# A gated broadcast on one core: input loads regrouped over two DMA queues, and one token shared between two engines

## The chip, the core and the metric

The kernel runs on one core of a Trainium2 chip. The metric is the device time of one execution, in microseconds (us), lower is better. Five runs of the kernel before took 93.67 to 93.85 us, with a median of 93.70 us.

## What is computed

```python
gate_weights = gate_weights / (np.sum(gate_weights, axis=-1, keepdims=True) + 1e-8)
output = x[:, :, None, :] * gate_weights[:, :, :, None]      # float32
```

`x` is 8 x 256 x 512 (4.2 MB), `gate_weights` is 8 x 256 x 8 (64 KB), and the output is 8 x 256 x 8 x 512 (33.6 MB). Every token's vector of 512 numbers is written out eight times, each time scaled by one normalised gate. There is one multiplication for every number that is written, and the output is eight times as large as the input.

## The kernel before

**Tiling.** The 2048 tokens are spread over 128 partitions, 16 tokens (`j` = 0 to 15) in each. "Token 3" below means the fourth token of every partition, 128 tokens in all. `x_all` holds all of x, `g_all` all gates, `gn` the normalised gates. `ring` is a buffer of 10 slots; a slot holds one finished token, 8 x 512 numbers in each partition.

**Loads (L46 to L48).** ScalarE's queue carries the gates. SyncE's queue carries x in two transfers: the head (tokens 0 to HEAD-1, with HEAD = 5, so 10,240 bytes in each partition), and then the rest (22,528 bytes in each partition). A queue issues its transfers in the order of the code. The profile calls SyncE's queue q1 and ScalarE's q10.

**Gates (L53 to L56).** VectorE sums the eight gates of each token, adds 1e-8, takes the reciprocal and multiplies. All work on tokens needs `gn`.

**Tokens (L70 to L87).** `CHUNKS` lists five chunks as (first token, number of tokens, first slot): tokens 0-1, 2-4, 5-7, 8-11 and 12-15. For each chunk the tokens are computed and one output transfer (L87) is issued on SyncE's queue. These transfers are called out1 to out5; they carry 4.2, 6.3, 6.3, 8.4 and 8.4 MB. A token is computed in one of three ways:

- tokens 0 and 1 are shared: three of the eight products on ScalarE (L63, 128x512 each) and five on VectorE (L65, 128x512 each);
- the first token of every later chunk (2, 5, 8, 12) goes to ScalarE, as eight products (L63);
- every other token is one VectorE instruction (L68, 128x4096).

A framework places the waits and orders each engine's instructions. Each transfer has its own semaphore, and a product waits until the whole transfer that brings its x has landed. Tokens 8 to 11 reuse the slots 0 to 3, so they wait until out1 and out2 have landed; tokens 12 and 13 reuse the slots 6 and 7 and wait for out3. The order on VectorE is by instruction, not by chunk: tokens 14 and 15, whose slots are fresh, come ahead of tokens 10 and 11.

Of the kernel before, what the change touches and what calls it, by code (L numbers as in the profile page):

```python
# [1 line left out]

# [4 lines left out]

SLOTS = 10
HEAD = 5
CHUNKS = ((0, 2, 0), (2, 3, 2), (5, 3, 5), (8, 4, 0), (12, 4, 6))  # L10


@with_exitstack
def kernel(
    ctx: ExitStack,
    tc: tile.TileContext,
    x: bass.AP,
    gate_weights: bass.AP,
    out: bass.AP,
):  # L20
    nc = tc.nc
    P = 128

    B, S, D = x.shape
    E = gate_weights.shape[-1]
    J = B * S // P

    fp32 = mybir.dt.float32
    mult = mybir.AluOpType.mult

    x_v = x.flatten_outer_dims().rearrange("(p j) d -> p j d", p=P)
    g_v = gate_weights.flatten_outer_dims().rearrange("(p j) e -> p j e", p=P)
    out_v = out.rearrange("b s e d -> (b s) e d").rearrange(
        "(p j) e d -> p j e d", p=P
    )

    pool = ctx.enter_context(tc.tile_pool(name="pool", bufs=1))

    g_all = pool.tile([P, J, E], fp32)
    x_all = pool.tile([P, J, D], fp32)  # L40
    ring = pool.tile([P, SLOTS, E, D], fp32)
    gsum = pool.tile([P, J, 1], fp32)
    gn = pool.tile([P, J, E], fp32)
    warm = pool.tile([P, 1], fp32)

    nc.scalar.dma_start(out=g_all, in_=g_v)  # L46
    nc.sync.dma_start(out=x_all[:, 0:HEAD, :], in_=x_v[:, 0:HEAD, :])
    nc.sync.dma_start(out=x_all[:, HEAD:J, :], in_=x_v[:, HEAD:J, :])  # L48

    nc.vector.memset(warm, 0.0)  # L50
    nc.scalar.copy(out=warm, in_=warm)  # L51

    nc.vector.reduce_sum(out=gsum, in_=g_all, axis=mybir.AxisListType.X)  # L53
    nc.vector.tensor_scalar_add(out=gsum, in0=gsum, scalar1=1e-8)  # L54
    nc.vector.reciprocal(out=gsum, in_=gsum)  # L55
    nc.vector.tensor_tensor(  # L56
        out=gn, in0=g_all, in1=gsum.to_broadcast([P, J, E]), op=mult
    )

    def scale_one(engine, j, e, slot):  # L60
        o_ap, s_ap = ring[:, slot, e, :], gn[:, j, e : e + 1]
        if engine is nc.scalar:
            nc.scalar.mul(out=o_ap, in_=x_all[:, j, :], mul=s_ap)  # L63
        else:
            nc.vector.tensor_scalar_mul(out=o_ap, in0=x_all[:, j, :], scalar1=s_ap)  # L65

    def scale_token(j, slot):
        nc.vector.tensor_tensor(  # L68
            out=ring[:, slot, :, :],
            in0=x_all[:, j : j + 1, :].to_broadcast([P, E, D]),  # L70
            in1=gn[:, j, :].unsqueeze(2).to_broadcast([P, E, D]),
            op=mult,
        )

    for j0, m, s0 in CHUNKS:
        for i in range(m):
            j, slot = j0 + i, s0 + i
            if j < 2:
                for e in range(E):
                    on_act = e < 3  # L80
                    scale_one(nc.scalar if on_act else nc.vector, j, e, slot)
            elif i == 0:
                for e in range(E):
                    scale_one(nc.scalar, j, e, slot)
            else:
                scale_token(j, slot)
        nc.sync.dma_start(  # L87
            out=out_v[:, j0 : j0 + m, :, :], in_=ring[:, s0 : s0 + m, :, :]
        )


# [1 line left out]
_INS = ['x', 'gate_weights']  # L93
_OUTS = [((8, 256, 8, 512), 'float32')]


# [23 lines left out]
```

## Time and profile before

| what | value |
|---|---|
| median of 5 runs | 93.70 us |
| the profiled execution's own time | 93.70 us |
| its span | 91.9 us |
| VectorE busy | 48.6 us (53%), 25 instructions |
| ScalarE busy | 25.1 us (27%), 40 instructions |
| bytes moved by DMA | 37.81 MB, mean 411 GB/s over the span |
| head of x landed (16 DMA engines) | 6.04 to 6.50 us |
| gates landed | 6.21 to 6.67 us |
| rest of x landed | 12.71 to 13.18 us |
| out1, out2, out3 landed (last of 16) | 23.14, 37.67, 52.21 us |
| out4, out5 landed (last of 16) | 71.75, 91.10 us |

Times are counted from the start of the span; 1.8 us of the execution's time lie outside it. A transfer is split over 16 DMA engines. Each of them moves its 8 partitions as 8 packets, one for each partition, and then sends a small packet that counts the landing. A transfer has landed when all 16 have. The trace holds a record of every packet, with its queue, its start and its duration; where the text speaks of packets, it reads those records.

### The profile page before, as it was taken

How to read it: one execution, taken by the hardware profiler on the slowest of the kernel's cores; microseconds unless marked ns; L12 is line 12 of the kernel's file. 1: busy time of each engine (PE TensorE's matmuls, PEld its weight loads, DVE VectorE, ACT ScalarE, POOL GpSimd, SP SyncE). 2: the span in 40 equal slices, each digit the busy share in tenths (PEclk: the TensorE clock that was granted, in tenths of full speed). 3: DMA queues.
4: the chain of work that ended last, by engine and by line, in shares of the span. 5: the costliest groups of instructions: out<-in, count | busy, mean ns of one | idle time of the engine just before them, and what ended most of it. 6: DMA issues, size and time to landing. Idle time of an engine off the chain costs nothing.

```text
span 91.9 us, 131 instructions
## 1 busy us (share of the span) xinstructions
DVE 48.6 (53%) x25; ACT 25.1 (27%) x40; POOL 0.2 (0%) x4
## 2 busy tenths in 40 slices
DVE  0009999999999999999999396000000000000000
ACT  5105999993892000000000299000000000000000
POOL 0000000000000000000000000000000000000000
DMA  3899989999778977997797999999982999999990
GB/s 54 355 494 402 392 385 456 456 456 570 342 342 385 642 342 342 578 449 342 342 684 342 456 456 456 456 456 456 456 371 114 428 456 456 456 456 456 456 456 0
DMA packets 1152, 37.81 MB, mean 411 GB/s; under 512 B 128, under 2 KB 256, under 8 KB 256
## 3 DMA queue, kind: packets, MB, share of 16 engines
q1 hardware_dynamic: 1008, 37.75, 95.9%
q10 hardware_dynamic: 144, 0.07, 0.3%
HBM read 4.26 MB, written 33.55 MB: 411 GB/s over the span
## 4 chain that ended last, share of the span: by engine, by line
DMA 31%; DVE 23%; ACT 5%; issue 2%; ACTq 1%; SPq 0%
DMA out_dram<-ring 25%; DVE ring L68 17%; DMA g_all<-in_gate_weights_dram 6%; ACT ring L63 5%; DVE ring L65 4%; ACTq L115 1%; DVE gn L56 0%; DVE gsum L53 0%; DVE gsum L55 0%; DVE gsum L54 0%; ACTq L63 0%; SPq L87 0%
## 5 line engine op out<-in xcount | busy, mean ns | idle before, releaser
L68 DVE TENSOR_TENSOR ring<-x_all,gn 128x4096 f32<-128x4096 f32 x10 | 43.5, 4419 | 1.4 <-DMA out_dram<-ring 1.4
L63 ACT ACTIVATE ring<-x_all,gn 128x512 f32<-128x512 f32 x38 | 23.6, 708 | 31.1 <-DMA out_dram<-ring 25.8
L65 DVE TENSOR_SCALAR ring<-x_all,gn 128x512 f32<-128x512 f32 x10 | 4.0, 480 | 0.0
L53 DVE TENSOR_REDUCE gsum<-g_all 128x16 f32<-128x128 f32 x1 | 0.3, 286 | 5.8 <-DMA g_all<-in_gate_weights_dram 5.8
L51 ACT ACT_TABLE_LOAD x1 | 1.3, 1283 | 1.1 <-PEq L104 1.1
L50 DVE MEMSET warm<- 128x1 f32 x1 | 0.1, 59 | 0.8 <-PEq L104 0.8
L56 DVE TENSOR_TENSOR gn<-g_all,gsum 128x128 f32<-128x128 f32 x1 | 0.3, 293 | 0.0
L55 DVE RECIPROCAL gsum<-gsum 128x16 f32<-128x16 f32 x1 | 0.3, 253 | 0.0
L51 ACT COPY warm<-warm 128x1 f32<-128x1 f32 x1 | 0.2, 193 | 0.0
L54 DVE TENSOR_SCALAR gsum<-gsum 128x16 f32<-128x16 f32 x1 | 0.2, 175 | 0.0
L104 POOL MEMSET const-bfloat16-1.0<- 128x1 bf16 x1 | 0.1, 102 | 0.0
L104 POOL MEMSET const-uint8-127<- 128x1 uint8 x1 | 0.1, 102 | 0.0
L104 POOL MEMSET const-float32-0.0<- 128x1 f32 x1 | 0.1, 101 | 0.2 <-issue 0.2
L104 POOL MEMSET const-float32-1.0<- 128x1 f32 x1 | 0.1, 99 | 0.0
## 6 DMA issues: line engine op xcount, KB each, us to landing
out_dram<-ring SPq DMA_DIRECT2D x2, 6144.0 KB, 20.0
out_dram<-ring SPq DMA_DIRECT2D x1, 4096.0 KB, 11.2
x_all<-in_x_dram SPq DMA_DIRECT2D x1, 2816.0 KB, 12.0
x_all<-in_x_dram SPq DMA_DIRECT2D x1, 1280.0 KB, 5.8
g_all<-in_gate_weights_dram ACTq DMA_DIRECT2D x1, 64.0 KB, 6.0
out_dram<-ring SPq DMA_DIRECT2D x2, 27.3
```

Of the source, the lines that this page charges most:

```text
L50: nc.vector.memset(warm, 0.0)
L51: nc.scalar.copy(out=warm, in_=warm)
L53: nc.vector.reduce_sum(out=gsum, in_=g_all, axis=mybir.AxisListType.X)
L54: nc.vector.tensor_scalar_add(out=gsum, in0=gsum, scalar1=1e-8)
L55: nc.vector.reciprocal(out=gsum, in_=gsum)
L56: nc.vector.tensor_tensor(out=gn, in0=g_all, in1=gsum.to_broadcast([P, J, E]), op=mult)
L63: nc.scalar.mul(out=o_ap, in_=x_all[:, j, :], mul=s_ap)
L65: nc.vector.tensor_scalar_mul(out=o_ap, in0=x_all[:, j, :], scalar1=s_ap)
L68: nc.vector.tensor_tensor(out=ring[:, slot, :, :], in0=x_all[:, j : j + 1, :].to_broadcast([P, E, D]), in1=gn[:, j, :].unsqueeze(2).to_bro ...
L104: nc = _bacc.Bacc("TRN2", target_bir_lowering=False, num_devices=1)
L115: with _tile.TileContext(nc) as tc:
```

## The change

HEAD becomes 2. The gates go first on SyncE's queue, the head of x (now tokens 0 and 1, 4,096 bytes in each partition) goes on ScalarE's queue, and the rest (now 14 tokens, 28,672 bytes in each partition) goes on SyncE's queue behind the gates. Tokens 2 to 4, which were in the head, are now in the rest. Token 2 stays on ScalarE. Token 3, which was one VectorE instruction, becomes eight: two products on ScalarE and six on VectorE. Token 4 stays one VectorE instruction. Chunks, slots and output transfers are as they were.

```diff
-HEAD = 5
+HEAD = 2
...
-    nc.scalar.dma_start(out=g_all, in_=g_v)
-    nc.sync.dma_start(out=x_all[:, 0:HEAD, :], in_=x_v[:, 0:HEAD, :])
+    nc.sync.dma_start(out=g_all, in_=g_v)
+    nc.scalar.dma_start(out=x_all[:, 0:HEAD, :], in_=x_v[:, 0:HEAD, :])
     nc.sync.dma_start(out=x_all[:, HEAD:J, :], in_=x_v[:, HEAD:J, :])
...
                     scale_one(nc.scalar if on_act else nc.vector, j, e, slot)
+            elif j == 2:
+                for e in range(E):
+                    scale_one(nc.scalar, j, e, slot)
+            elif j == 3:
+                for e in range(E):
+                    scale_one(nc.scalar if e < 2 else nc.vector, j, e, slot)
             elif i == 0:
                 for e in range(E):
                     scale_one(nc.scalar, j, e, slot)
```

## The prediction, made before the changed kernel was timed

> **What bounds the kernel now.** I read the page's slices first, then the issues, then the packet records at the places where one transfer follows another.
>
> On the page, the DMA row of the slices, the queues and the issues:
>
> ```profile
> DMA  3899989999778977997797999999982999999990
> q1 hardware_dynamic: 1008, 37.75, 95.9%
> q10 hardware_dynamic: 144, 0.07, 0.3%
> out_dram<-ring SPq DMA_DIRECT2D x1, 4096.0 KB, 11.2
> x_all<-in_x_dram SPq DMA_DIRECT2D x1, 2816.0 KB, 12.0
> x_all<-in_x_dram SPq DMA_DIRECT2D x1, 1280.0 KB, 5.8
> g_all<-in_gate_weights_dram ACTq DMA_DIRECT2D x1, 64.0 KB, 6.0
> ```
>
> The DMA engines are full from the second slice to the last: SyncE's queue alone takes 95.9% of their time. VectorE (53%) and ScalarE (27%) have slack. A digit below 9 is mostly a packet straddling a slice, so a gap has to be looked for in the records. The chain of waits ends with ScalarE's last work at 57.3 us, which is misleading: out4 and out5 are queued by then and run for another 34 us.
>
> Timeline (start, duration, what):
>
> ```profile
> 0.72 0.39 ACTq L46 DMA_DIRECT2D g_all<-in_gate_weights_dram  x1
> 0.73 0.38 SPq L47 DMA_DIRECT2D x_all<-in_x_dram  x1
> 1.16 0.42 SPq L48 DMA_DIRECT2D x_all<-in_x_dram  x1
> 6.70 0.29 DVE L53 TENSOR_REDUCE gsum<-g_all 128x16 f32<-128x128 f32 x1 [5.84 <-DMA g_all<-in_gate_weights_dram]
> 7.84 13.60 ACT L63 ACTIVATE ring<-x_all,gn 128x512 f32<-128x512 f32 x22 [5.21 <-DVE gn L56]
> 7.84 4.05 DVE L65 TENSOR_SCALAR ring<-x_all,gn 128x512 f32<-128x512 f32 x10
> 11.81 39.10 DVE L68 TENSOR_TENSOR ring<-x_all,gn 128x4096 f32<-128x4096 f32 x9
> 11.98 45.69 SPq L87 DMA_DIRECT2D out_dram<-ring  x5
> ```
>
> The first output is issued at 11.98. The loads need the DMA engines until almost 13 us, so that issue is nearly hidden. The DMA view of 12.3 to 13.0 us in 40 slices shows by how little:
>
> ```profile
> GB/s 0 0 0 0 0 0 0 0 0 0 0 0 0 0 0 0 0 0 0 0 0 0 0 0 0 0 0 0 0 0 7490 5617 0 5617 1872 3745 1872 1872 1872 0
> DMA packets 32, 0.52 MB, mean 749 GB/s; under 512 B 16, under 2 KB 16, under 8 KB 16
> ```
>
> A packet counts in the slice where it starts. The sixteen small packets are the ends of the x load, from 12.35 to 12.82 us by the records; the sixteen large ones are the first of out1, starting at 12.83 to 12.98. So fifteen DMA engines idle for up to 0.5 us, and the sixteenth, done with x at 12.82, does not. From there every engine moves at its own fixed pace: 1.22 us for 32,768 bytes, 1.82 for 49,152, 2.42 for 65,536, each packet starting where the one before ends. One more gap follows: out3's last packets end at 51.68 to 51.86, and out4, issued at 50.98, begins at 51.84 to 51.98, again about 0.86 us behind its issue (to the first engine). Out2 and out5 are issued long ahead. The end is the latest engine's, so only what moves the latest engine counts.
>
> **The loads.** Bytes are unchanged. An engine's eight packets of the head repeat every 382 ns at 10,240 bytes, a 512-byte gate packet adds 24 ns, a 22,528-byte packet of the rest repeats every 833. The first packets start at 1.74 to 2.57 but nearly all end at 2.77 to 3.14, so full rate begins, in effect, near 2.85 - 0.385 = 2.46. Then 8 x (382 + 24) + 8 x 833 = 9.91 us, ending at 12.37. After: on the line through 27 ns (512 bytes) and 385 (10,240), a 4,096-byte packet costs 0.159 and repeats in 0.156; 28,672 bytes repeat in 1.059. Gates and head end at 2.46 + 8 x (0.024 + 0.156) = 3.90, the rest at 3.90 + 8 x 1.059 = 12.37: the same. The latest engine was 0.45 us later than that, by small stalls between 4 and 5 us which I carry over: 12.82. The start-up isn't priced by any row for so small a packet. If the small first packets do not stall, data flows from 1.74 instead of 2.46: -0.7. If they stall as long but carry only 0.03 us of data meanwhile instead of 0.385: +0.36. I take 0, since the bytes and most packet ends point to one common release near 2.5 us, whatever the packet.
>
> **When out1 is issued.** Gates land 0.53 us behind their last packet (6.14 to 6.67), the head 0.35. From there to `gn`: 7.84 - 6.67 = 1.17. So `gn` is ready at about 3.9 + 0.53 + 1.17 = 5.6 (was 7.84), and the five VectorE products of each of two tokens take 4.05 as before, with ScalarE's 6 x 0.618 = 3.7 beside them. Out1 is issued at 5.6 + 4.05 + 0.09 = 9.75 instead of 11.98. Its cover: the loads until 12.37 to 12.82. So 2.2 us of earlier compute give only the gap: the latest engine starts out1 at 12.83 instead of 12.98, **-0.15**.
>
> **Tokens 2 to 4** wait for the rest, 13.18 (its landing before), instead of running from 11.8. VectorE idles from 9.7 until then. Chunk 2: ScalarE 10 x 0.618 = 6.2, to 19.4; VectorE 6 x 0.405 + 4.344 = 6.8, to 20.0 (39.10/9 = 4.344). Out2 is issued near 20.05 instead of 20.63 and is needed 0.86 us ahead of 22.60, where out1 ends: 1.7 us of cover, cost nothing. If token 3 stayed whole on VectorE, 13.18 + 8.69 = 21.9 would have left none, so the sharing is what pays for the smaller head. Two more 128x512 products on ScalarE (40, was 38) lie in its idle time.
>
> **Out4.** VectorE then has no wait until eight 128x4096 instructions are done: 13.18 + 2.43 + 8 x 4.344 = 50.4 instead of 50.9. Out4 is issued at 50.4 and ready at 51.3, ahead of out3's end: its latest engine starts at 51.87 instead of 51.98, **-0.11**.
>
> Sum: 93.70 - 0.15 - 0.11 = 93.44, **93.4 us**. The profiled execution took 93.70, the median itself.
>
> **One rule against the row.** In 2.75 to 3.75 us the packets of the two queues come one by one in turn:
>
> ```profile
> q1 hardware_dynamic: 37, 0.38, 91.8%
> q10 hardware_dynamic: 39, 0.02, 6.6%
> ```
>
> 37 large against 39 small: a queue with a small packet waits for one large one of the other queue. The Trainium skill (DMA: Bandwidth & Descriptors, Queues, rings and completion order) has a DMA engine drain about 9 to 17 descriptors of a queue before it turns to the next; by that, all eight head packets would go in one turn, the second rival below would cost nothing, and the sum would stay 93.4. By the row it can cost microseconds. The same page (Issuing engines are not separate DMA queues) says that a second issuing queue saves only issue time; by that alone the loads end as before, as in my sum.
>
> **Rivals.** (1) *The loads end later, or out1's start was hidden anyway*: the latest engine had no gap (12.82 to 12.83). With a start-up worse by 0.15 to 0.36, the sum is 93.6 to 93.8. For: nothing in the trace is like the new start. Against: equal bytes.
>
> (2) *The head gets stuck behind the rest; slower.* Gates and rest share q1; the head is alone on q10. Eight gate packets pair with eight head packets only if both queues begin together. All sixteen engines began with q1 before, though ScalarE issued 10 ns earlier, so q1 leads by something under 0.4 us. Gate packets last 24 ns, so a lead lets them run out, and each of L head packets left over then waits for one 28,672-byte packet, 1.06 us. The head's end is 3.9 + 1.06 L, and out1's latest start follows it by 0.35 + 0.02 + 4.05 + 0.09 + 1.0 = 5.5. Against 12.98 this decides from 7.5 us, that is L over 3.4. L = 4 gives 94.2, L = 6 gives 96.4, L = 8 gives 98.5. Against it: the slow start, up to 2.5 us, gives q10 time to arrive; L up to 3 costs nothing.
>
> (3) *The start gets faster*: the first packets no longer stall, 92.7 to 93.1.
>
> (4) *Out2 is late*: the rest lands over 1.7 us later, or chunk 2 takes that much longer. Each us beyond costs one. 94 to 95.
>
> **Numbers.** Forecast 93.2 to 93.6: 0.50, of which 0.40 is faster by over 0.2% (under 93.51; 0.2% is about what a measurement of this kernel can tell from no change) and 0.10 within it. Rival 1: 0.18 (0.16 same, 0.02 slower). Rival 2: 0.20, slower. Rival 3: 0.07, faster. Rival 4: 0.05, slower. Faster 0.47, same 0.26, slower 0.27. The range is 93.0 to 96.0: it leaves out about 0.04 below and 0.10 above (L of 6 to 8). The forecast's own range is 93.2 to 93.6.
>
> **What would show it.** Right: the head landed by 4.5 us, `gn` by 5.7, out1 issued near 9.8, out1's first packets starting where the x load's end, with no gap; out2 issued near 20, out4 near 50.4 with no gap at 51.8. Wrong: head packets of q10 in the records after 5 us (rival 2: a DMA gap between 12.8 us and out1), x landing away from 13.2 (rivals 1 and 3), a gap near 22.6 (rival 4), or VectorE's wait moved from the gates to the head.

## The result: slower by 0.3%

The changed kernel takes 94.01 us in the median (93.58 to 94.49, 31 runs), the kernel before 93.69 us (93.51 to 94.25, 52 runs). The ratio is 1.0034, with a 95% interval of 1.0024 to 1.0043. The forecast was 93.44, faster; the time lies inside the range of 93.0 to 96.0, but the sign was wrong. The profiled execution of the changed kernel took 93.85 us, 0.16 below its median, so the profile shows a somewhat milder case than the typical run.

The timeline of the changed kernel (start, duration, what):

```profile
4.17 0.29 DVE L53 TENSOR_REDUCE gsum<-g_all 128x16 f32<-128x128 f32 x1 [3.32 <-DMA g_all<-in_gate_weights_dram]
5.32 4.05 DVE L65 TENSOR_SCALAR ring<-x_all,gn 128x512 f32<-128x512 f32 x10
9.46 48.51 SPq L93 DMA_DIRECT2D out_dram<-ring  x5
13.78 16.05 ACT L63 ACTIVATE ring<-x_all,gn 128x512 f32<-128x512 f32 x26 [4.67 <-DMA x_all<-in_x_dram]
13.78 2.47 DVE L65 TENSOR_SCALAR ring<-x_all,gn 128x512 f32<-128x512 f32 x6 [4.41 <-DMA x_all<-in_x_dram]
16.16 34.77 DVE L68 TENSOR_TENSOR ring<-x_all,gn 128x4096 f32<-128x4096 f32 x8
```

The gates come 2.5 us earlier and out1 is issued at 9.46 instead of 11.98, as planned. But work on the rest of x begins at 13.78, not at the expected 13.2. The issues, with the time from issue to landing, say the same:

```profile
out_dram<-ring SPq DMA_DIRECT2D x1, 4096.0 KB, 14.1
x_all<-in_x_dram SPq DMA_DIRECT2D x1, 3584.0 KB, 12.6
x_all<-in_x_dram ACTq DMA_DIRECT2D x1, 512.0 KB, 3.9
g_all<-in_gate_weights_dram SPq DMA_DIRECT2D x1, 64.0 KB, 3.4
```

Head plus rest is the same bytes as before, and before they were all in at 13.18. The packet records show where the load lost its time. On each DMA engine the rest is eight packets of 28,672 bytes. The first six take about the 1.06 us that the prediction worked out (1.14 at most). The seventh takes 1.06 to 1.58 us, the eighth 1.25 to 1.80, so the load's packets end at 12.95 to 13.48 us. Summed over the eight packets an engine is 0.69 us over 1.062 each; this sum is called *the excess* below.

The records do not name the engine, so "the latest engine" here and below is the last of the sixteen at each point, not always the same one. For it, out1 starts at 13.49 instead of 12.98 (+0.51). From there to the end of out3 it takes 38.68 us instead of 38.88 (-0.20). Out4 follows without a gap, where the kernel before had 0.12. With out4 and out5 0.02 shorter, that is +0.17; the last packets end at 90.92 instead of 90.76, and the two profiled executions differ by 0.15.

### The profile page after: what moved, and what is told of

The parts are those of the page before. It is cut to its first block, busy times and chain, and to the rows that moved or that the text cites. A ratio compares the mean times of both kernels' runs of the same rounds, so it can differ in the third digit from the quotient of the medians.

```text
span 92.1 us, 139 instructions
## 1 busy us (share of the span) xinstructions
DVE 46.7 (51%) x30; ACT 26.3 (29%) x42; POOL 0.2 (0%) x4
## 4 chain that ended last, share of the span: by engine, by line
DMA 39%; DVE 15%; ACT 5%; issue 2%; ACTq 1%; SPq 0%
DMA out_dram<-ring 25%; DMA x_all<-in_x_dram 14%; DVE ring L68 13%; ACT ring L63 5%; DVE ring L65 3%; ACTq L121 1%; SPq L46 0%; ACTq L63 0%; SPq L93 0%
## 5 line engine op out<-in xcount | busy, mean ns | idle before, releaser
L68 DVE TENSOR_TENSOR ring<-x_all,gn 128x4096 f32<-128x4096 f32 x9 | 39.2, 4421 | 1.7 <-DMA out_dram<-ring 1.7
L63 ACT ACTIVATE ring<-x_all,gn 128x512 f32<-128x512 f32 x40 | 24.9, 709 | 30.1 <-DMA out_dram<-ring 22.8
L65 DVE TENSOR_SCALAR ring<-x_all,gn 128x512 f32<-128x512 f32 x16 | 6.5, 483 | 4.4 <-DMA x_all<-in_x_dram 4.4
```

Source lines behind the costliest of these rows:

```text
L68: nc.vector.tensor_tensor(out=ring[:, slot, :, :], in0=x_all[:, j : j + 1, :].to_broadcast([P, E, D]), in1=gn[:, j, :].unsqueeze(2).to_bro ...
```

## Experiments

Theory **T1**: an output transfer that is queued behind the load while the load still runs slows the load's last packets; the change did this by making out1 early. Rivals: **T2**, the larger packets slow down by themselves; **T3**, the swap of the queues does it. Time ratios are to runs of the kernel before that were taken together with each experiment, with the 95% interval.

### 1. Out1 later, the same loads

```diff
-                    on_act = e < 3
+                    on_act = False
```

> Edit: the change as it is, but tokens 0 and 1 wholly on VectorE (16 products instead of 10), so that out1 is issued about 2.4 us later, near 11.9 instead of 9.46, with the same loads. Theory T1 (an output that is queued behind the x load while that load still runs slows the load's last packets): the last two 28,672-byte packets of each engine are back at 1.06 us each, the x load's packets end at 12.3 to 12.8 instead of 12.95 to 13.48, its landing is near 13.15 instead of 13.75, out4 is issued near 50.4, and the time is 93.4 to 93.6. Rival T2 (the larger packets of the rest slow down by themselves near 10 us, whatever is queued): the last two packets stay at 1.25 to 1.8 us, landing stays near 13.75, time 93.9 to 94.1.

Measured: 93.33 us, ratio 0.9968 (0.9953 to 0.9984). Out1 was issued at 12.50, later than the 11.9 expected, since the gates also came later in this execution. No packet but one exceeds 1.07 us (that one 1.11, and it is a sixth); the seventh and eighth all take 1.062; the excess is 0.004 us. T2 falls. The profiled execution itself took 94.05, far above the median: on four of the sixteen engines the rest began up to 5.03 us, a packet later than elsewhere, and ended at 13.2 to 13.50, with every packet at its pace. So its landing says nothing on T1, its packet durations do.

### 2. The queues undone

The gates go back to ScalarE's queue and the head to SyncE's; HEAD = 2 and the shared token 3 stay.

```diff
-    nc.sync.dma_start(out=g_all, in_=g_v)
-    nc.scalar.dma_start(out=x_all[:, 0:HEAD, :], in_=x_v[:, 0:HEAD, :])
+    nc.scalar.dma_start(out=g_all, in_=g_v)
+    nc.sync.dma_start(out=x_all[:, 0:HEAD, :], in_=x_v[:, 0:HEAD, :])
```

> Edit: the two queues swapped back (gates on ScalarE's queue, head of two tokens and rest on SyncE's); HEAD = 2 and the shared token 3 stay. T1 (out1 queued during the x load slows its last packets): out1 is issued near 9.5 as in the change, so the last two packets are slow again, x lands near 13.7, time 93.9 to 94.1. Rival T3 (the swap itself costs, gates running ahead of the head on the same queue): the loads end at 12.8, time 93.4 to 93.6. T2 (large packets slow by themselves): as T1.

Measured: 93.14 us, ratio 0.9942 (0.9930 to 0.9954), clearly faster than both kernels; the excess is 0.025 us. This was the outcome foretold for T3 (the loads end at 12.78; the time is even below T3's 93.4 to 93.6), not for T1. But there is a second difference: without the swap the gates land later, and out1 is issued at 10.06 instead of 9.46.

### 3. The sharing alone

HEAD = 5 and the queues as before; only token 3 is shared.

> Edit: loads as in the kernel before (HEAD = 5, gates on ScalarE's queue); only token 3 is shared. All theories: x load and out1 as before (out1 issued at 12.0, x landed at 13.2, packets of 0.836 us), out2 issued near 18.7 instead of 20.6, out4 near 49.1 instead of 51.0, so the small gap ahead of out4 goes: 0.1 us, 93.5 to 93.7.

Measured: 93.55 us, ratio 0.9982 (0.9972 to 0.9992), as expected. The load has no excess; out1 is issued at 12.08. The latest engine passes from out3 to out4 without a gap (51.96 to 51.97).

### 4. The sharing undone

The branch for token 3 is taken out of the changed kernel.

> Edit: the change's loads, token 3 whole on VectorE as before. All theories: out1 at 9.46 and slow last packets of x as in the change; VectorE does nine 128x4096 instructions from 13.8, so out2 is issued near 22.5 and out4 near 52.9, each later than the transfer ahead of it ends; gaps of some 0.3 and 1.2 us, time 95.2 to 95.8. If the time stays near 94.0, the sharing carried nothing.

Measured: 95.62 us, ratio 1.0213 (1.0193 to 1.0232). The line that shows why is VectorE's:

```profile
13.61 39.11 DVE L68 TENSOR_TENSOR ring<-x_all,gn 128x4096 f32<-128x4096 f32 x9 [4.21 <-DMA x_all<-in_x_dram]
```

Nine instructions from 13.61 end at 52.7, and out4 waits for the last: 1.19 us pass between the end of out3 and the start of out4 on the latest engine. Ahead of out2 there is a gap too, 0.47 us, because two of the nine instructions come before it. So the sharing is worth 1.6 us beside the smaller head. The excess is there again, 0.55 us, with out1 at 9.49.

### 5 to 8. Is it the swap, or when out1 is issued?

Run 5: the change, out1 as two transfers of one token.

```diff
+            if j0 == 0:
+                nc.sync.dma_start(
+                    out=out_v[:, j : j + 1, :, :], in_=ring[:, slot : slot + 1, :, :]
+                )
-        nc.sync.dma_start(
-            out=out_v[:, j0 : j0 + m, :, :], in_=ring[:, s0 : s0 + m, :, :]
-        )
+        if j0 > 0:
+            nc.sync.dma_start(
+                out=out_v[:, j0 : j0 + m, :, :], in_=ring[:, s0 : s0 + m, :, :]
+            )
```

> Edit: the change, with out1 issued as two transfers of one token each, the first about 2 us earlier (near 7.45 us), the second at 9.46 as before. T1 (an output queued behind the running x load slows the load): the slow packets begin earlier, near 9 to 10 us, and add up to as much or more; x lands at 13.75 or later, time 94.0 to 94.6. If only the position counts (the last two packets of the load, whatever the time of the issue): packets 1 to 6 at 1.06 us as in the change, the last two slow, x lands near 13.75, time 94.0. T3 (the swap of the queues causes it, not out1): as the change, 94.0.

Measured: 94.43 us, ratio 1.0085 (1.0071 to 1.0099). The first half is issued at 7.34; the excess rises to 1.22 us, and x lands at 14.06. Packets 1 to 6 stay within 0.02 us of their pace in the mean, the seventh takes 1.70 and the eighth 1.61. More loss, as T1 has it, but not earlier.

Run 6: the change with one setting moved, queues still swapped.

```diff
-                    on_act = e < 3
+                    on_act = e < 2
```

> Edit: the change, with 12 instead of 10 of the products of tokens 0 and 1 on VectorE, so that out1 is issued 0.8 us later, near 10.3, and the queues stay swapped. T1: the load's excess shrinks from 0.67 us per engine to below 0.2, x lands near 13.2, time 93.2 to 93.5, like the kernel with the queues undone, whose out1 came at 10.06. T3 (swap): last two packets stay slow, x lands near 13.7, time 93.9 to 94.1.

Measured: 93.07 us, ratio 0.9936 (0.9923 to 0.9950); excess 0.14 us. The swap is there, out1 is 0.67 us later than in the change, and the loss is nearly gone:

```profile
5.19 2.56 ACT L63 ACTIVATE ring<-x_all,gn 128x512 f32<-128x512 f32 x4 [2.56 <-DVE gn L56]
5.19 4.84 DVE L65 TENSOR_SCALAR ring<-x_all,gn 128x512 f32<-128x512 f32 x12
10.13 47.50 SPq L93 DMA_DIRECT2D out_dram<-ring  x5
```

Two instructions more on the path ahead of the first output make the kernel 1% faster than the change.

Run 7: the queues undone as in run 2, and out1 in two as in run 5.

> Edit: HEAD = 2 and shared token 3 with the queues as before (the variant that ran in 93.14), and out1 as two transfers of one token, the first issued near 8.0 us, the second near 10.06. T1: now the slow packets appear here too, x lands at 13.4 or later, time 93.5 to 94.1. T3 (the swap causes the slow packets): none appear, x lands at 13.1, time 93.1 to 93.2.

Measured: 94.66 us, ratio 1.0105 (1.0090 to 1.0121); excess 1.31 us, the first half issued at 7.84. That is more than the 93.5 to 94.1 that I had expected of T1. The load's last packet ends at 14.05 and x lands at 14.33. The loss appears without the swap and (run 6) vanishes with it: T3 falls as the cause of the slow packets, and T1 stands, with an edge near 10 us that run 2 happened to lie behind.

A rival that none of the theories names is that the load slows while VectorE and ScalarE stand idle. The stretch from 10 to 13 us in the change (first line) and in run 2 (second line) speaks against it. After the stretch and its length come the busy time of VectorE, ScalarE and GpSimd, the clock, the share of the DMA engines' time and the GB/s; a packet counts where it starts:

```profile
10.00:13.00 3.00, 0.00 (x0) 0.00 (x0) 0.00 (x0) 1.00 1.01 339
10.00:13.00 3.00, 0.00 (x0) 0.00 (x0) 0.00 (x0) 1.00 1.12 481
```

Both engines are idle in both kernels, and only the change has the excess. Run 5 also has the change's work on tokens 0 and 1 (from 5.17 instead of 5.32 us, equally long) and differs in the output alone.

Run 8: the swap and the shared token with HEAD = 5.

> Edit: the change with HEAD = 5: only the queues are swapped and token 3 shared. T1: the head lands near 6.3, out1 is issued near 10.6, late enough to leave the load alone; x lands near 13.2, out2 is issued near 17.5, time 93.2 to 93.5. T3 (swap costs by itself): slow last packets of x, 93.8 or more.

Measured: 93.96 us, ratio 1.0030 (1.0019 to 1.0042). My expectation failed: the time is T3's, without T3's slow packets (excess 0.001). Out1 is issued at 12.36, not 10.6, because the head landed late:

```profile
x_all<-in_x_dram ACTq DMA_DIRECT2D x1, 1280.0 KB, 7.4
g_all<-in_gate_weights_dram SPq DMA_DIRECT2D x1, 64.0 KB, 4.6
```

The head of five tokens takes 7.4 us instead of 5.8, though the gates are early. The DMA view of 5.0 to 6.4 us in the same kernel:

```profile
q1 hardware_dynamic: 17, 0.38, 63.4%
q10 hardware_dynamic: 21, 0.22, 36.1%
```

On q1 the gates are finished and seventeen packets of the rest (17 x 22,528 bytes = 0.38 MB) have started, while q10 still starts 21 packets of the head. By the records the first packet of the rest starts at 5.13 to 5.69 on the sixteen engines, the last head packets start as late as 6.52, and the second packet of the rest only after those. On fifteen of the sixteen engines one head packet was left to wait for that one packet of the rest. This is the prediction's second rival, with L of about 1, in a kernel whose head is larger. Out1's first packets start at 13.21 to 13.36, 0.47 behind the load's end at the least; in run 3, with the same HEAD, they started at 12.92 to 13.07. So the swap has a price of its own here, by another path. In the changed kernel each engine also had head packets left when its gates were done (the gates' closing packets start at 3.13 to 3.83 us, the head's 0.47 later, the time of three head packets). They ran back to back ahead of the rest, whose first packet ends at 4.67 at the earliest while the last head packet starts at 4.15, so there the swap had no price by this path.

### 9 and 10. Is it the last two packets, or the last microseconds?

Run 9: the change with the last token of x as a load of its own.

```diff
-    nc.sync.dma_start(out=x_all[:, HEAD:J, :], in_=x_v[:, HEAD:J, :])
+    nc.sync.dma_start(out=x_all[:, HEAD : J - 1, :], in_=x_v[:, HEAD : J - 1, :])
+    nc.sync.dma_start(out=x_all[:, J - 1 : J, :], in_=x_v[:, J - 1 : J, :])
```

> Edit: the change, with the last token of x as a load of its own at the end of the queue, so the last eight packets of the load are 2,048 bytes each and the eight ahead of them 26,624 (nominally about 0.98 us). T1a (only the last two packets ahead of a queued output are slowed, counted in packets): the slow ones are now small, all 26,624-byte packets keep their pace, x lands near 13.2, time 93.0 to 93.3, though out1 is issued at 9.46 as in the change. T1b (the last 2 to 3 us of the load are slowed, counted in time or bytes): the last two 26,624-byte packets are slow, x lands near 13.7, time 93.9 to 94.1.

Measured: 93.91 us, ratio 1.0020 (1.0010 to 1.0030); excess 0.67 us as in the change, spread over the last 26,624-byte packet (mean 1.23 for 0.987) and the first small ones (0.26 and 0.18 for 0.08).

Run 10: run 7 with the same small last load.

> Edit: the variant with the queues as before and out1 in two transfers (94.66 us), with the last token of x as a load of its own. Its outputs are queued from about 8.7 us, long before the large packets end. T1a (counted in packets): its loss of 1.2 us per engine falls to below 0.3, time 93.1 to 93.4. T1b (time or bytes): the loss stays, time 94.4 to 94.7.

Measured: 94.51 us, ratio 1.0074 (1.0061 to 1.0087); excess 1.17 us. In both runs the loss falls on the last large packet and the small ones behind it, not on the last two packets of the load, so T1a, counted in packets, falls. A queued load does no comparable harm: the small last load was queued behind the large one from 1.6 us on, and the large packets kept their pace within 4% in the mean until some 10.5 us. In the kernel before, where the rest of x was queued behind the head, the last four of each engine's eight head packets took 0.385 to 0.400 us in the mean, at a pace of 0.385.

### 11. The best version

Run 2 with 12 instead of 10 products of tokens 0 and 1 on VectorE.

> Edit: HEAD = 2 and shared token 3, queues as before, and 12 instead of 10 products of tokens 0 and 1 on VectorE, so that out1 is issued near 10.9: after the last x packet but one has begun on every engine and 0.9 us ahead of the load's first end. T1a and T1b alike: no slow packet at all and no gap, x lands near 13.1, 93.0 to 93.2; it should be no slower than either of the two best so far (93.07, 93.14).

Measured: 93.10 us, ratio 0.9935 (0.9923 to 0.9947); excess 0.02 us. It is level with runs 2 and 6; the 0.14 us of excess in run 6's profile shows in no difference of the medians. That profiled execution took 93.38 us, the longest of run 6's five and 0.31 above their median, so its excess need not be typical. The lines of run 11:

```profile
5.92 4.84 DVE L65 TENSOR_SCALAR ring<-x_all,gn 128x512 f32<-128x512 f32 x12
10.85 46.42 SPq L93 DMA_DIRECT2D out_dram<-ring  x5
13.15 16.04 ACT L63 ACTIVATE ring<-x_all,gn 128x512 f32<-128x512 f32 x26 [4.67 <-DMA x_all<-in_x_dram]
```

Here the rest of x is usable at 13.15 us, where the prediction had put it.

### 12. One early output, not split

> Edit: the change, but of the eight products of tokens 0 and 1 only two are computed (VectorE); the other six are left out and those parts of the ring are set to zero ahead of time, on VectorE and GpSimd. So out1, one transfer as in the change, is issued about 2.4 us earlier, near 7.0. T1b with full price (the last 2 to 3 us of the load are slowed whenever an output is queued before them, and the change at 9.46 took only a part of it): the last two packets add up to about 1.2 us excess as in the runs with two output transfers, none of the earlier packets are much slower, x lands near 14.2, time 94.3 to 94.6. If the excess stays at 0.67 us and the time at 94.0, splitting out1 into smaller packets, not the earlier issue, had raised the price. If packets 3 to 6 are slow as well, the loss counts from the issue.

This kernel leaves out six of the eight products of tokens 0 and 1, so that part of its output is zeros; it serves the measurement alone. Measured: 94.45 us, ratio 1.0073 (1.0055 to 1.0090); out1 issued at 7.15, excess 1.36 us, packets 1 to 6 at their pace, the seventh at 1.83 and the eighth at 1.65 in the mean. The full price needs no splitting. The issue and the two engines that wait for the load:

```profile
7.15 51.49 SPq L94 DMA_DIRECT2D out_dram<-ring  x5
14.47 2.47 DVE L67 TENSOR_SCALAR ring<-x_all,gn 128x512 f32<-128x512 f32 x6 [7.41 <-DMA x_all<-in_x_dram]
14.54 16.03 ACT L65 ACTIVATE ring<-x_all,gn 128x512 f32<-128x512 f32 x26 [11.90 <-DMA x_all<-in_x_dram]
```

The earliest output of all makes everything behind the load 1.3 us later.

The slow packets can be seen in the DMA view of 8 to 14.5 us in 40 slices. A packet counts in the slice where it starts. Run 11 first, then run 12:

```profile
GB/s 1235 1059 176 176 0 0 1059 1235 353 176 0 0 176 1235 1059 176 176 0 0 1059 1059 529 176 0 0 202 1412 1210 202 202 0 0 0 1210 1210 605 202 0 0 0
GB/s 1412 529 176 529 0 0 882 1235 176 353 176 0 176 1235 706 176 529 0 0 0 0 0 0 0 706 1059 706 353 0 0 0 0 0 0 202 1613 1210 202 0 0
```

In run 11 a group of packets starts every six or seven slices (1.06 us), the outputs following the load. In run 12 the third group, the seventh packets, starts at its time, and the next group comes only eleven or twelve slices later.

### The runs in the order of the first output's issue

| run | first output issued (us) | excess per DMA engine (us) | median time (us) | ratio to before |
|---|---|---|---|---|
| 12, six of eight products left out | 7.15 | 1.36 | 94.45 | 1.0073 |
| 5, out1 in two | 7.34 | 1.22 | 94.43 | 1.0085 |
| 7, in two, queues undone | 7.84 | 1.31 | 94.66 | 1.0105 |
| 10, as 7, small last load | 8.00 | 1.17 | 94.51 | 1.0074 |
| 9, change with small last load | 9.32 | 0.67 | 93.91 | 1.0020 |
| the change | 9.46 | 0.69 | 94.01 | 1.0034 |
| 4, sharing undone | 9.49 | 0.55 | 95.62 | 1.0213 |
| 2, queues undone | 10.06 | 0.03 | 93.14 | 0.9942 |
| 6, change, 12 products | 10.13 | 0.14 | 93.07 | 0.9936 |
| 11, queues undone, 12 products | 10.85 | 0.02 | 93.10 | 0.9935 |
| before | 11.98 | 0.00 | 93.69 | 1 |
| 3, sharing alone | 12.08 | 0.00 | 93.55 | 0.9982 |
| 8, swap with HEAD = 5 | 12.36 | 0.00 | 93.96 | 1.0030 |
| 1, out1 late | 12.50 | 0.00 | 93.33 | 0.9968 |

Issue and excess are of the profiled executions, one for each run. Three levels: full price (1.17 to 1.36 us) for issues up to 8.0, about half (0.55 to 0.69) at 9.3 to 9.5, nearly none (0.14 at most) from 10.06 on.

The slow stretch itself begins late, however early the output is queued. In run 12 it begins with the seventh packets, which start at 10.07 to 10.70 us, when each engine has 57 KB of the load left. In the change it begins with the seventh on ten engines, and on the other six only with the eighth, from 11.42 us on. In runs 9 and 10 it is mostly the last large packet and the small ones behind it, 43 KB.

Where nothing held an output up (out1 before and in runs 1 and 8), its first packets started some 0.85 us behind its issue. Counted by that, outputs ready by 8.85 us paid in full, those ready at 10.2 to 10.3 paid half, and those ready from 10.9 on almost nothing. The change lies in between. Where an execution lands on this slope may be why the 31 times of the change spread from 93.58 to 94.49, but run 1, without excess, spreads from 93.19 to 94.05 in 12 runs; so that is a reading, not shown.

## Why the prediction was wrong

**What bounds the kernel**: right. The DMA engines are full in every run but for short gaps (the longest is run 4's 1.19 us), and each time is told by the latest engine's packets.

**The loads**: right up to 10 us, wrong after it. The start-up was taken as unchanged; head and gates ended and the rest started near 3.6 to 4.3 (worked out: 3.9), the large packets took 1.062 (worked out: repeat in 1.059). At that pace to the end, the engine that started the rest last, at 4.31, would have been the last to end, at 4.31 + 8 x 1.059 = 12.78. The forecast was 12.82; the last engine in fact ended at 13.48.

**The step that failed** is the one that said of out1's earlier issue: "Its cover: the loads until 12.37 to 12.82. So 2.2 us of earlier compute give only the gap". It priced the early issue as hidden, because the queue serves its transfers in order. The records do show order: as the sixteen engines' loads end, from 12.95 to 13.48 us, the first output packets start one by one, from 12.96 to 13.49, none ahead of its turn. But the load slows down while an output waits behind it. In place of -0.15 the latest engine's out1 start moved by +0.51. Nothing in the profile of before could show this, since out1's packets became ready only as the load ended; the prediction bounded the start-up, which the trace did not show, and did not bound this overlap, which it did not show either.

**Tokens 2 to 4, sharing**: right; run 4 gives it 1.6 us. **Out4**: right in kind. Its issue was forecast at 50.4 and came at 51.00, late by the load's delay (in run 2, without that delay, at 50.36); the latest engine has no gap there.

**The sum without the failed step** is seen in runs 2, 6 and 11: 93.07 to 93.14, against 93.44. The direction is as worked out and the size is larger. In run 2 the latest engine's out1 starts at 12.78 (-0.20, forecast -0.15), the gap ahead of out4 is gone (-0.12, forecast -0.11), and the outputs took less time, which was not forecast: -0.20 over out1 to out3, where the packets themselves were shorter, and -0.13 over out4 and out5. Of the latter only 0.02 is in the mean packet (2.4252 instead of 2.4265 us); meanwhile the sixteen engines drew together from 0.28 to 0.16 us apart. Together -0.65, and the profiled executions differ by 93.70 - 93.05 = 0.65.

**Rivals**: the first had the loads end later by a worse start-up. They did end later, but the rest began as worked out. The third (a faster start) and the fourth (out2 late) did not occur; out2 follows out1 without a gap in the change. The second (head stuck behind the rest) did not decide the change, and did occur in run 8. The upper part of the range of 93.0 to 96.0 was there for this second rival, so it is luck that the time lies inside it. Run 8 also answers the rule that the prediction had weighed. The Trainium skill (DMA: Bandwidth & Descriptors, Queues, rings and completion order) would have a DMA engine take about 9 to 17 descriptors of a queue in one turn, so eight head packets would not be parted by a packet of the rest. In run 8 a single 22,528-byte packet goes between two head packets on fifteen engines, so there q1's turn was one packet, as in the row of the kernel before. But one by one in turn is not the whole rule either: in the change three head packets ran back to back behind the gates' end, though the rest had been issued at 1.15 us on the other queue. The prediction had priced each such packet at a wait of 1.06 us; here they waited for none.

**What stays open** is why a queued output slows the load. The records show no output packet before the load's end, and the outputs then run at their usual pace (1.213 us for 32,768 bytes), so they do not show what takes the time from the load. No run separates the reading from the writing side, and the output was not tried on another queue beside the load.

## What to carry to other kernels

Work that is hidden behind a transfer need not be free when it ends in another transfer on the same engines: price not only when an issue is needed but also what it runs beside once it is early. When an undo of one part is faster than both versions, look at what that part moved in time before blaming the part: here the swap did harm by bringing the gates, and so the first output, 0.6 us forward. A series of issue times settled what a list of parts could not.

## What the runs showed of the hardware that was not expected

- An output queued behind a running load cost the load up to 1.36 us in the mean of the 16 DMA engines (run 12). There the seventh packet took 1.83 us in the mean instead of 1.062, which is 16 x 28,672 bytes / 1.83 us = 251 GB/s instead of 432. A load queued behind a load did nothing comparable (runs 9 and 10, and the kernel before).
- DMA engines in step are a little slower than DMA engines out of step. Where a gap let all sixteen start out1 within 0.15 to 0.16 us (before, runs 1, 3, 8), 32,768-byte packets took 1.224 us in the mean and 49,152-byte packets 1.822; where they ran on from the load with 0.53 to 0.62 us between the first and the last (the change, runs 2, 11, 12), they took 1.213 and 1.815. Over out1 to out3 that is 8 x 0.011 + 16 x 0.007 = 0.2 us. Run 4 has both in one execution: out1, with 0.61 us between the engines, took 1.213 per packet; behind the gap ahead of out2 they were 0.15 apart, and the 49,152-byte packets took 1.823. That being in step is the cause is still a reading: no run set the offset alone, and for 65,536-byte packets the order does not hold (2.423 in run 3 at 0.16 us apart, 2.426 in the change at 0.34).
- A late DMA engine stays late: in run 2 the 0.62 us between the first and the last engine at the load's end is still 0.62 where out3 begins. A gap for all but the latest engine then evens it out (0.60 to 0.28 ahead of out4).
